# An LRU layer whose first three blocks share their chunks, with the adaLN sums dealt out between the matmuls

## The chip, the cores and the metric

The kernel runs on one core of a Trainium2 chip. The metric is the device time of one execution in microseconds (us), as the median of several runs. "Engines" are TensorE (PE), VectorE (DVE), ScalarE (ACT), GpSimd (POOL) and SyncE (SP, which here only issues transfers).

## What is computed

The model has two layers over 1024 latent tokens (D = 1024); the first also reads 256 context tokens. Layer 0 mixes tokens with a bidirectional gated linear recurrence (RG-LRU), layer 1 with long convolutions (Hyena); each is followed by a squared-ReLU MLP. Every sub-layer has an RMS norm with shift, scale and gate from the condition vector (adaLN). The change lies in layer 0 and in the start of the program:

```python
mod = cond @ ada_w[i] + ada_b[i]          # six vectors of 1024: j = 0..5
u = rms_norm(x, g) * (1 + scale) + shift
z = u @ w_in + b_in                        # 1024 x 2048
gate = gelu(z[..., :W])                    # "Z"
xl = row_conv(z[..., W:], conv_w, conv_b)  # "X", and the same for the context
r = sigmoid(xl @ w_a + b_a); i = sigmoid(xl @ w_i + b_i)   # "U", two directions, 4 heads of 256
log_a = -8 * r * softplus(-lam)
a = exp(log_a); bx = sqrt(-expm1(2 * log_a)) * i * xl      # "A"
h = linear_scan(a, bx, h0)                 # "S", forward and backward
y = ((h_f + h_b) * gate) @ w_out + b_out   # "Y"
h = sin(freq * (h @ fw + fb))              # Hyena's filter network, three steps, then h @ fw4
```

## The kernel before

**Precision.** Each fp32 product is made from a high and a low part of both operands, in three matmuls (`mm3`, lines L133 to L135). A weight block of 128x1024 is loaded by `load` (L111) into a buffer `raw`, ACT casts it to `whi` (L113), DVE subtracts to get `wlo` (L115). There are two `raw` buffers.

**Blocks.** Channels go in 8 blocks of 128, as four heads h with two halves m. The list `TOKENS` names the work by letter and block. `X` multiplies the normed input with one weight block, adds the convolution on DVE (L485) and splits the result into `xh` (ACT, L505) and `xl` (DVE, L507). `Z` makes the gelu gate. `U` makes the four sigmoid gates of one block from both halves of a head. `A` makes tanh and exp on ACT and the products on DVE and POOL. `S` takes the square roots, runs two scans on DVE (L588 into the tile `hf`, L591), combines them with the gate on POOL (L590, L592, L594), and writes `hf` to DRAM as `yd` (L596). There is one `hf` buffer.

**Sums.** `E` makes one of the six adaLN vectors (j = 2, 3, 4): eight loads `eraw` of 128x1024 (L615, in the two `raw` buffers), eight multiply-adds on DVE into `eacc` (L617, L619; `eacc` lies in the buffer of `hf`), and 8 matmuls of one column to sum over partitions (L622, each shown as two by the profile). In the list before, each of the three stands as one token between two blocks: `E20` ahead of Z00, `E30` ahead of U00, `E40` ahead of A00.

**Order.** A scheduler places the instructions of all tokens on the engines from its own estimates; within an engine, work is done in the placed order. All loads, and the writes `yd`, stand in SP's one queue. ACT's activations that need a table follow each other in program order (`table`).

**Start.** The program first makes the Hyena filter's features (sines, L302 to L312), the two adaLN vectors j = 0, 1 that the first norm needs (`ada_first`: 16 loads, 32 matmuls, L172), the norm's statistics of the three chunks (two of 512 latent columns, one of 256 context columns), and then scales and splits each chunk (L256 to L260). It also splits the filter network's last weight `fw4` and writes the parts to DRAM (`w4d`), from where the MLP part of layer 0 fetches them again.

Of the kernel before, what the change touches and what calls it, by code (L numbers as in the profile page):

```python
# [46 lines left out]
def tile_block(ctx: ExitStack, tc: tile.TileContext, a, out, dbg=None):  # L47
# [47 lines left out]
    w4d = dram.tile([4, P, 2, 512], F32, name="w4d")  # L95
# [190 lines left out]
    def filter_pos(fp, fb, aside):  # L286
# [13 lines left out]
        for n in range(3):  # L300
# [12 lines left out]
            aside(n)  # L313
        tap("fh3", h)
# [8 lines left out]
        hp = fp.tile([P, 16, 4, 32], F32, tag="hp", name="hp")  # L323
# [11 lines left out]
        for n, t in enumerate(split(fb, "hps", hp.rearrange("p g j t -> p (g j t)"), [P, 2048], 1, "v")):  # L335
            nc.sync.dma_start(hpd[:, :, n].rearrange("g p c -> p g c"), t.bitcast(F32).rearrange("p (g c) -> p g c", g=16))

    def filter_w4(fp, fb):
        fw4 = fp.tile([P, 2048], F32, tag="fw4", name="fw4")
        nc.sync.dma_start(fw4, a["fw4"])  # L340
        for n, t in enumerate(split(fb, "w4s", fw4, [P, 2048], 1)):
            nc.sync.dma_start(w4d[:, :, n].rearrange("u p c -> p u c"), t.bitcast(F32).rearrange("p (u c) -> p u c", u=4))

    def filters(fp):
# [78 lines left out]
    def x_load(pool):  # L423
        xt = []
        for c, src, o, n in ((0, "xT", 0, 512), (1, "xT", 512, 512), (2, "ctxT", 0, TC)):
            xt.append([pool.tile([P, n], F32, tag=f"x{c}{k}", name=nm("xl"), bufs=1) for k in range(NT)])
            for k in range(NT):
                nc.sync.dma_start(xt[c][k], a[src][k * P:(k + 1) * P, o:o + n])
        return xt

    TOKENS = ("X00 X01 E20 Z00 E30 U00 E40 A00 X10 S00 Z01 U01 A01 X11 S01 "
# [4 lines left out]
    def lru(load, open_x, npool, close_n, xt, rs):  # L436
# [6 lines left out]
        with ExitStack() as st:  # L443
# [30 lines left out]
            for tag, dt, w, n in (("z", F32, T + TC, 1), ("xc", F32, T + TC, 3), ("g", F32, T, 2), ("R", F32, T + TC, 2), ("I", F32, T + TC, 2),  # L474
                                  ("xl2", F32R, T + TC, 1), ("T", F32, T + TC, 2), ("hf", F32, T, 1)):
                lt.tile([P, w], dt, tag=tag, name=nm(tag), bufs=n)
# [14 lines left out]
            def X(h, m):  # L491
# [3 lines left out]
                for c in (0, 1, 2) if dt < 2 else (2, 0, 1):  # L495
# [3 lines left out]
                    nc.scalar.activation(z[:, cols[c]], p, AF.Identity, bias=vcol("lru_b_in", 8 + dt))  # L499
                x_ = lt.tile([P, T + TC], F32, tag="xc", name=nm("xc"), bufs=3)  # L500
# [9 lines left out]

            def Z(h, m):
# [18 lines left out]
            def U(h, m):  # L530
# [4 lines left out]
                for e in range(2):  # L535
                    pcx = None
                    tl = []
                    for ai in range(2):
# [14 lines left out]
                        tl.append(r)  # L553
                    rs_.append(tl)
# [55 lines left out]
            def E(j, _):  # L610

                acc = lt.tile([P, T], F32, tag="hf", name=nm("eacc"), bufs=1)
                for k in range(NT):
# [775 lines left out]
```

## Time and profile before

| | us |
|---|---|
| median of 3 runs | 2873.65 (2871.66 to 2874.5) |
| the profiled execution | 2870.54 |
| its span, first to last instruction | 2868.8 |
| PE busy | 2680.0 (93%) |
| DVE busy | 1605.5 (56%) |
| ACT busy | 1098.6 (38%) |

The span is what the profile's rows divide; the profiled execution's own time lies 1.74 us above it, and 3.11 us below the median. Busy shares are means over the whole program: the stages of layer 0 that the change touches fill the first tenth of it, and have to be read by themselves.

### The profile page before, as it was taken

How to read it: one execution, taken by the hardware profiler on the slowest of the kernel's cores; microseconds unless marked ns; L12 is line 12 of the kernel's file. 1: busy time of each engine (PE TensorE's matmuls, PEld its weight loads, DVE VectorE, ACT ScalarE, POOL GpSimd, SP SyncE). 2: the span in 40 equal slices, each digit the busy share in tenths (PEclk: the TensorE clock that was granted, in tenths of full speed). 3: DMA queues.
4: the chain of work that ended last, by engine and by line, in shares of the span. 5: the costliest groups of instructions: out<-in, count | busy, mean ns of one | idle time of the engine just before them, and what ended most of it. 6: DMA issues, size and time to landing. Idle time of an engine off the chain costs nothing.

```text
span 2868.8 us, 29759 instructions
## 1 busy us (share of the span) xinstructions
PE 2680.0 (93%) x11298; PEld 2071.4 (72%) x11298; DVE 1605.5 (56%) x2193; ACT 1098.6 (38%) x1670; POOL 245.2 (9%) x154
## 2 busy tenths in 40 slices
PE   6789889999999999999999997778799999999998
PEld 1677777788777777788787763334488888888887
DVE  7666575875555555444833368768576333333336
ACT  6457667542333233322522244444434211122213
POOL 0223432100000000000100021112001000000000
PEclk8799999999999999999999999998899999999999
DMA  8431123344444434322313254455321111111112
GB/s 304 125 111 44 52 66 121 102 145 133 121 114 138 122 114 138 100 68 63 123 52 118 67 159 122 134 159 169 120 87 45 52 52 44 52 44 52 51 46 96
DMA packets 121794, 288.60 MB, mean 101 GB/s; under 512 B 11883, under 2 KB 28269, under 8 KB 121395
## 3 DMA queue, kind: packets, MB, share of 16 engines
q1 hardware_dynamic: 116578, 275.42, 31.6%
q0 software_dynamic: 3344, 9.18, 1.0%
q10 hardware_dynamic: 1728, 2.10, 0.2%
q8 instruction: 89, 1.46, 0.2%
q14 instruction: 55, 0.44, 0.0%
HBM read 215.08 MB, written 37.75 MB: 88 GB/s over the span
## 4 chain that ended last, share of the span: by engine, by line
PE 72%; DVE 11%; DMA 9%; ACT 6%; issue 2%; SPq 0%; POOL 0%; DVEq 0%; ACTq 0%; POOLq 0%
PE ps L152 52%; PE ps L134 4%; PE ps L133 4%; PE ps L135 4%; DMA e<-big 3%; DMA adaw<-in_ada_w_dram 2%; PE ps L396 2%; PE ps L928 1%; DVE xc L485 1%; DMA big<-e 1%; DMA eraw<-in_ada_w_dram 1%; DVE hf L588 1%; PE ps L822 1%; PE ps L947 1%; ACT r L525 1%
## 5 line engine op out<-in xcount | busy, mean ns | idle before, releaser
L152 PE MATMUL ps<-u,whi 128*128 128x512 f32 x2696 | 734.7, 394 | 0.0
L113 ACT CAST whi<-raw 128x1024 fp32r<-128x1024 f32 x206 | 216.3, 1050 | 1113.5 <-PE ps L152 1007.4
L152 PEld LDWEIGHTS ps<-u,whi 128*128 128x128 f32 x2696 | 505.1, 188 | 113.5 <-issue 7.4
L115 DVE TENSOR_TENSOR wlo<-raw,whi 128x1024 fp32r<-128x1024 f32 x206 | 261.9, 1271 | 467.8 <-ACT whi L113 467.0
L152 PE MATMUL ps<-u,wlo 128*128 128x512 f32 x1348 | 418.9, 390 | 0.0
L152 PE MATMUL ps<-hh,whi 128*128 128x512 f32 x896 | 296.7, 409 | 0.0
L152 PEld LDWEIGHTS ps<-u,wlo 128*128 128x128 f32 x1348 | 253.1, 188 | 53.0 <-DVE wlo L115 0.7
L152 PE MATMUL ps<-hh,wlo 128*128 128x512 f32 x896 | 282.1, 390 | 0.0
L152 PE MATMUL ps<-hl,whi 128*128 128x512 f32 x896 | 280.5, 390 | 0.0
L152 PEld LDWEIGHTS ps<-hh,whi 128*128 128x128 f32 x896 | 168.4, 188 | 51.3 <-issue 17.3
L134 PE MATMUL ps<-u,whi 128*128 128x512 f32 (+1 forms) x508 | 195.2, 385 | 3.5 <-POOL u L260 2.9
L133 PE MATMUL ps<-u,whi 128*128 128x512 f32 (+1 forms) x508 | 186.9, 385 | 11.5 <-ACT u L259 11.5
L745 DVE SCALAR_TENSOR_TENSOR big<-ps,mod,big 128x512 f32<-128x512 f32 (+1 forms) x132 | 91.7, 731 | 185.3 <-PE ps L152 177.7
L135 PE MATMUL ps<-u,wlo 128*128 128x512 f32 (+1 forms) x508 | 193.0, 382 | 1.8 <-DVE wlo L115 1.8
L152 PEld LDWEIGHTS ps<-hl,whi 128*128 128x128 f32 x896 | 168.3, 188 | 36.1 <-issue 1.0
L152 PEld LDWEIGHTS ps<-hh,wlo 128*128 128x128 f32 x896 | 168.2, 188 | 34.9
L745 DVE SCALAR_TENSOR_TENSOR x<-ps,mod,x 128x512 f32<-128x512 f32 x128 | 91.3, 746 | 145.1 <-PE ps L152 137.2
L195 DVE SCALAR_TENSOR_TENSOR acc<-adaw,cond,acc 128x512 f32<-128x512 f32 x98 | 73.6, 751 | 93.1 <-DMA adaw<-in_ada_w_dram 92.2
L260 POOL TENSOR_TENSOR u<-nu,u 128x512 fp32r<-128x512 f32 x24 | 33.9, 1413 | 1021.8 <-ACT u L259 1012.6
L133 PEld LDWEIGHTS ps<-u,whi 128*128 128x128 f32 x508 | 97.8, 193 | 29.9 <-ACT u L259 12.2
L134 PEld LDWEIGHTS ps<-u,whi 128*128 128x128 f32 x508 | 97.9, 193 | 25.4 <-POOL u L260 6.0
L135 PEld LDWEIGHTS ps<-u,wlo 128*128 128x128 f32 x508 | 97.4, 192 | 20.1 <-DVE wlo L115 3.0
(242 smaller groups left out, 4051.2 us busy)
## 6 DMA issues: line engine op xcount, KB each, us to landing
raw<-in_mlp_w_dram SPq DMA_DIRECT2D x136, 512.0 KB
adaw<-in_ada_w_dram SPq DMA_DIRECT2D x112, 256.0 KB
fd<-fe SPq DMA_DIRECT2D x64, 256.0 KB
big<-e SPq DMA_DIRECT2D x64, 256.0 KB
ft<-fd SPq DMA_DIRECT2D x64, 256.0 KB
e<-big SPq DMA_DIRECT2D x64, 256.0 KB
eraw<-in_ada_w_dram SPq DMA_DIRECT2D x24, 512.0 KB
raw<-in_hy_w_in_dram SPq DMA_DIRECT2D x24, 512.0 KB
```

The source lines that it names most:

```text
L113: lsplit[0] = nc.scalar.copy(hi, raw)
L115: lsplit[1] = nc.vector.tensor_tensor(lo, raw, hi.bitcast(F32), op=ALU.subtract)
L133: first = pin(nc.tensor.matmul(ps, wh, rh, start=start, stop=False))
L134: pin(nc.tensor.matmul(ps, wh, rl, start=False, stop=False))
L135: pin(nc.tensor.matmul(ps, wl, rh, start=False, stop=stop))
L152: nc.tensor.matmul(pp[c], x, y[c][k], start=first, stop=last)
L195: nc.vector.scalar_tensor_tensor(acc, w, s, acc, op0=ALU.mult, op1=ALU.add)
L260: applied[k % 2] = (nc.vector if k % 2 else nc.gpsimd).tensor_tensor(ul[k], u, uh[k].bitcast(F32), op=ALU.subtract)
L396: nc.tensor.matmul(p2, mf[:, 1 if g == 0 else 0], st.pop(("ht", i)), start=True, stop=True)
L485: eng.scalar_tensor_tensor(ov[:, :, so], zv[:, :, si], vcol("lru_conv_w", 8 * tap_ + dt), ov[:, :, so], op0=ALU.mult, op1=ALU.add)
L525: ins = nc.scalar.activation(*args, **kw)
L745: nc.vector.scalar_tensor_tensor(xs[m][:, cs], ps[:, :n], g2[:, m:m + 1], xs[m][:, cs], op0=ALU.mult, op1=ALU.add)
```

## The change

- The first three blocks, X00, X01 and Z00, become one token `B`: the three weight blocks are loaded ahead, and for each chunk the matmuls of the three blocks alternate. The context's X follow last.
- Each `E` becomes eight single steps. `estep()` stands after each chunk of an X or Z, after each pair of gates in U, and once after B; it issues the next step of those that are due. The eight steps of j = 2 are due from the start, those of j = 3 after S00, those of j = 4 after S01; what is left before an S is issued there.
- X puts the context's chunk first for all blocks.
- At the start, x is loaded ahead of the adaLN weights, statistics and scaling are written chunk by chunk, and the matrix of filter features (`filter_mat`) is assembled behind the norm, its low part on POOL.
- `fw4` is no longer split at the start; `fetch` in the MLP loads the raw quarter and splits it there.

The core of the diff (lines of the changed kernel are shifted by up to 60):

```diff
@@ -332,14 +334,13 @@
                 for j in range(4):
                     eng = nc.scalar.copy if j % 2 else nc.vector.tensor_copy
                     eng(dst[:, :, m, j, 16 * half:16 * half + 16], src[:, :, m, j, :])
-        for n, t in enumerate(split(fb, "hps", hp.rearrange("p g j t -> p (g j t)"), [P, 2048], 1, "v")):
+        hph = fp.tile([P, 2048], F32R, tag="hph", name="hph")
+        for q in range(4):
+            cs = slice(512 * q, 512 * q + 512)
+            nc.scalar.copy(hph[:, cs], hpr[:, cs].bitcast(F32))
+            nc.gpsimd.tensor_tensor(hpr[:, cs], hpr[:, cs].bitcast(F32), hph[:, cs].bitcast(F32), op=ALU.subtract)
+        for n, t in enumerate((hph, hpr)):
             nc.sync.dma_start(hpd[:, :, n].rearrange("g p c -> p g c"), t.bitcast(F32).rearrange("p (g c) -> p g c", g=16))
-
-    def filter_w4(fp, fb):
-        fw4 = fp.tile([P, 2048], F32, tag="fw4", name="fw4")
...
@@ -353,7 +354,10 @@

         def fetch(u):
             w = fp.tile([P, 2, 512], F32R, tag="w4", name=nm("w4"), bufs=2)
-            nc.sync.dma_start(w.bitcast(F32), w4d[u])
+            raw = fp.tile([P, 512], F32, tag="fe", name=nm("w4r"), bufs=2)
+            nc.sync.dma_start(raw, a["fw4"][:, u * 512:(u + 1) * 512])
+            nc.scalar.copy(w[:, 0], raw)
+            nc.vector.tensor_tensor(w[:, 1], raw, w[:, 0].bitcast(F32), op=ALU.subtract)
             st["w4", u] = w

...
-    TOKENS = ("X00 X01 E20 Z00 E30 U00 E40 A00 X10 S00 Z01 U01 A01 X11 S01 "
...
+    TOKENS = ("B00 U00 A00 X10 S00 Z01 U01 A01 X11 S01 "
               "Z10 U10 A10 X20 S10 Z11 U11 A11 X21 S11 "
...
@@ -446,9 +450,24 @@
                 uh[c], ul[c] = ([utile(s_, c) for _ in range(NT)] for s_ in "hl")
             both = [utile("", 2) for _ in range(NT)]
             uh[2], ul[2] = [t[:, :TC] for t in both], [t[:, TC:] for t in both]
-            for c, n in ((0, 512), (1, 512), (2, TC)):
+            xt = x_tiles(npool)
+            with ExitStack() as fst:
+                fs = fst.enter_context(tc.tile_pool(name="fs", bufs=1, reuse_waits="tile"))
+                first = ada_first(fs, wp_[0])
+                h = filter_pos(fs)
+                x_load(xt, 0)
+                for step in first:
+                    step()
+                make_scale(scl[:, 0], vcols("norm_g", 0, 8), mod[:, 0, 1])
+                make_scale(sclc, vcols("norm_g", 0, 8), modc[:, 1])
+                w0 = [load(a["lru_w_in"][m]) for m in (8, 9, 0)]
+                for c in (1, 2):
+                    x_load(xt, c)
                 with tc.high_priority():
-                    norm_apply(npool, lambda k: xt[c][k], rs[c], n, scl[:, 0] if c < 2 else sclc, mod[:, 0, 0] if c < 2 else modc[:, 0], uh[c], ul[c], True)
+                    for c, n in ((0, 512), (1, 512), (2, TC)):
+                        r = norm_stats(npool, lambda k: xt[c][k], n, npool)
+                        norm_apply(npool, lambda k: xt[c][k], r, n, scl[:, 0] if c < 2 else sclc, mod[:, 0, 0] if c < 2 else modc[:, 0], uh[c], ul[c], True)
+                filter_mat(fs, h)
             close_n()

             sp8 = up.tile([P, 2, 16], F32, name="sp8")
...
                 dt = 2 * h + m
                 w = load(a["lru_w_in"][8 + dt])
                 z = lt.tile([P, T + TC], F32, tag="z", name=nm("z"), bufs=1)
-                for c in (0, 1, 2) if dt < 2 else (2, 0, 1):
+                for c in (2, 0, 1):
                     ps = psum()
                     p = ps if c < 2 else ps[:, :TC]
                     gemm(p, w, 0, uh[c], ul[c], range(NT), NT)
                     nc.scalar.activation(z[:, cols[c]], p, AF.Identity, bias=vcol("lru_b_in", 8 + dt))
+                    estep()
+                mix(h, m, z)
+
...
+            def B(h, m):
+
+                zz = [lt.tile([P, T + TC], F32, tag=t, name=nm("z"), bufs=n) for t, n in (("z", 1), ("xc", 3))]
+                g = lt.tile([P, T], F32, tag="g", name=nm("g"), bufs=2)
+                GT[0, 0] = g
+                for c in range(3):
+                    n = 3 if c < 2 else 2
+                    pp = [psum() for _ in range(n)]
+                    pp = [p if c < 2 else p[:, :TC] for p in pp]
+                    for k in range(NT):
+                        for i in range(n):
+                            gemm(pp[i], w0[i], 0, uh[c], ul[c], [k], NT)
+                    for i in range(2):
+                        nc.scalar.activation(zz[i][:, cols[c]], pp[i], AF.Identity, bias=vcol("lru_b_in", 8 + i))
+                    if c < 2:
+                        table(g[:, cols[c]], pp[2], AF.Gelu_apprx_tanh, bias=vcol("lru_b_in", 0))
+                for i in range(2):
+                    mix(0, i, zz[i])
+                estep()
+
...
@@ -516,6 +560,7 @@
                     ps = psum()
                     gemm(ps, w, 0, uh[c], ul[c], range(NT), NT)
                     table(g[:, cols[c]], ps, AF.Gelu_apprx_tanh, bias=vcol("lru_b_in", dt))
+                    estep()
                 GT[h, m] = g


...
                         tl.append(r)
+                        estep()
                     rs_.append(tl)
                 RW[h, m] = rs_
...
-            def E(j, _):
-
-                acc = lt.tile([P, T], F32, tag="hf", name=nm("eacc"), bufs=1)
-                for k in range(NT):
-                    w = wp_[0].tile([P, 1024], F32, tag="raw", name=nm("eraw"), bufs=2)
-                    nc.sync.dma_start(w, a["ada_w"][0, k * P:(k + 1) * P, j * D:(j + 1) * D])
-                    if k == 0:
-                        nc.vector.tensor_scalar(acc, w, cond[:, 0, k:k + 1], None, op0=ALU.mult)
-                    else:
-                        nc.vector.scalar_tensor_tensor(acc, w, cond[:, 0, k:k + 1], acc, op0=ALU.mult, op1=ALU.add)
+
+            eacc = {}
+
+            def E(j, k):
+                if k == 0:
+                    eacc[j] = lt.tile([P, T], F32, tag="hf", name=nm("eacc"), bufs=1)
+                acc = eacc[j]
+                w = wp_[0].tile([P, 1024], F32, tag="raw", name=nm("eraw"), bufs=2)
+                nc.sync.dma_start(w, a["ada_w"][0, k * P:(k + 1) * P, j * D:(j + 1) * D])
+                if k == 0:
+                    nc.vector.tensor_scalar(acc, w, cond[:, 0, k:k + 1], None, op0=ALU.mult)
+                else:
+                    nc.vector.scalar_tensor_tensor(acc, w, cond[:, 0, k:k + 1], acc, op0=ALU.mult, op1=ALU.add)
+                if k < NT - 1:
+                    return
                 ps = psum_st()
                 for t in range(8):
                     nc.tensor.matmul(ps[:, t:t + 1], acc[:, t * P:(t + 1) * P], ones[:, 0:1], start=True, stop=True)
@@ -624,8 +675,20 @@
                 if j == 4:
                     make_scale(scl[:, 1], vcols("norm_g", 8, 8), mod[:, 0, 4])

-            for tok in TOKENS.split():
-                dict(E=E, X=X, Z=Z, U=U, A=A, S=S, Y=Y)[tok[0]](int(tok[1]), int(tok[2]))
+            etodo = [(2, k) for k in range(NT)]
+
+            def estep():
+                if etodo:
+                    E(*etodo.pop(0))
+
+            for i, tok in enumerate(TOKENS.split()):
+
+                if tok[0] == "S":
+                    while etodo:
+                        estep()
+                dict(B=B, X=X, Z=Z, U=U, A=A, S=S, Y=Y)[tok[0]](int(tok[1]), int(tok[2]))
+                if tok in ("S00", "S01"):
+                    etodo.extend((3 + int(tok[2]), k) for k in range(NT))

         xs = open_x()
         late = [2, 3, 4, 5, 6, 7, 0, 1]
```

What the scheduler makes of it, at three places that matter below.

**Place 1: the loads and the write of S00.** SP's queue before, from the weights of X10 on (in order those of X10, Z01, U01's gates, X11, Z10 and U10's gates, `raw_1161` to `raw_1615`, then `yd_78`, the result of S00):

```order
L111 DMA raw_1161<-in_lru_w_in_dram 128x1024
L111 DMA raw_1270<-in_lru_w_in_dram 128x1024
L111 DMA raw_1329<-in_lru_w_g_dram 128x1024
L111 DMA raw_1447<-in_lru_w_in_dram 128x1024
L111 DMA raw_1556<-in_lru_w_in_dram 128x1024
L111 DMA raw_1615<-in_lru_w_g_dram 128x1024
L596 DMA yd_78<-hf_1263 128x1024
L111 DMA raw_1733<-in_lru_w_in_dram 128x1024
```

SP's queue of the changed kernel, from the weights of Z01 on (`yd_77` is the result of S00, `raw_1257` the gate weights of U01, `eraw` the loads of the sum j = 3, `raw_1387` the weights of X11):

```order
L110 DMA raw_1191<-in_lru_w_in_dram 128x1024
L664 DMA eraw_1225<-in_ada_w_dram 128x1024
L664 DMA eraw_1254<-in_ada_w_dram 128x1024
L642 DMA yd_77<-hf_1184 128x1024
L110 DMA raw_1257<-in_lru_w_g_dram 128x1024
L664 DMA eraw_1288<-in_ada_w_dram 128x1024
L664 DMA eraw_1315<-in_ada_w_dram 128x1024
L664 DMA eraw_1343<-in_ada_w_dram 128x1024
L664 DMA eraw_1370<-in_ada_w_dram 128x1024
L110 DMA raw_1387<-in_lru_w_in_dram 128x1024
L664 DMA eraw_1420<-in_ada_w_dram 128x1024
```

The gate weights of U01 (`raw_1329` before, `raw_1257` now) stood ahead of the write of S00's result, with three more weight blocks between; now they stand behind that write and behind two loads of the sum.

On DVE, the scans of S00 before (`xl_1257` belongs to X10, the two `wlo` to the weights of X11 and Z10):

```order
L586 SCALAR_TENSOR_TENSOR T_1147<-r_1013,r_1038 128x256
L115 TENSOR_TENSOR wlo_1451<-raw_1447,whi_1449 128x1024
L588 SCALAR_TENSOR_TENSOR hf_1263<-r_1013,T_1147,r_1038 128x1024
L485 SCALAR_TENSOR_TENSOR xc_1246<-z_1167,vec,xc_1246 128x16x62
L591 SCALAR_TENSOR_TENSOR T_1149<-r_1062,r_1087 128x1280
L485 SCALAR_TENSOR_TENSOR xc_1246<-z_1167,vec,xc_1246 128x16x63 x2
L507 TENSOR_TENSOR xl_1257<-xc_1246,xh_1255 128x1280
L115 TENSOR_TENSOR wlo_1560<-raw_1556,whi_1558 128x1024
```

and in the changed kernel, the same scans, up to the gate weights of U01 (`wlo_1261`):

```order
L631 TENSOR_TENSOR r_967<-r_967,T_1049 128x1280
L632 SCALAR_TENSOR_TENSOR T_1049<-r_939,r_967 128x256
L634 SCALAR_TENSOR_TENSOR hf_1184<-r_939,T_1049,r_967 128x1024
L504 SCALAR_TENSOR_TENSOR xc_1167<-z_1069,vec,xc_1167 128x16x62
L504 SCALAR_TENSOR_TENSOR xc_1167<-z_1069,vec,xc_1167 128x16x63
L637 SCALAR_TENSOR_TENSOR T_1051<-r_994,r_1022 128x1280
L504 SCALAR_TENSOR_TENSOR xc_1167<-z_1069,vec,xc_1167 128x16x63
L531 TENSOR_TENSOR xl_1178<-xc_1167,xh_1176 128x1280
L666 TENSOR_SCALAR eacc_1224<-eraw_1225,cond 128x1024
L668 SCALAR_TENSOR_TENSOR eacc_1224<-eraw_1254,cond,eacc_1224 128x1024
L114 TENSOR_TENSOR wlo_1261<-raw_1257,whi_1259 128x1024
```

The first step of the sum (`eacc_1224`) has come between the scans and the split of U01's gate weights; `eraw_1225` is in the buffer into which `raw_1257` goes, and `eacc_1224` in the one that `hf_1184` has.

**Place 2: the end of a U.** ACT's order before, at the end of U01 (`r` are the sigmoids, `T` the first tanh of A01, `whi_1617` the gate weights of U10):

```order
L525 ACTIVATE r_1409<-ps_1410,vec 128x512
L525 ACTIVATE r_1409<-ps_1418,vec 128x512
L113 CAST whi_1617<-raw_1615 128x1024
L525 ACTIVATE r_1409<-ps_1401,vec 128x256
L525 ACTIVATE T_1433<-r_1335,sp_633 128x1280
L525 ACTIVATE T_1435<-r_1384,sp_633 128x1280
```

and in the changed kernel at the same place (`whi_1514` are the weights of Z10):

```order
L570 ACTIVATE r_1346<-ps_1347,vec 128x512
L570 ACTIVATE r_1346<-ps_1355,vec 128x512
L112 CAST whi_1514<-raw_1512 128x1024
L570 ACTIVATE r_1346<-ps_1335,vec 128x256
L570 ACTIVATE T_1373<-r_1263,sp_643 128x1280
L570 ACTIVATE T_1375<-r_1318,sp_643 128x1280
```

In both, the cast of a weight block stands ahead of U01's last sigmoid and of A01's tanh. The load of that block was the fourth transfer on SP's queue behind Z01's weights (`raw_1270`); it is now the twelfth behind Z01's weights (`raw_1191`): the write of S00's result and all eight loads of the sum stand between.

**Place 3: the column sums of the first E.** PE's order before, at the end of X01 (`ps_839` are X01's context columns, `ps_920` and `ps_946` the first chunks of Z00):

```order
L133 MATMUL ps_839<-u_500,whi_782 128x256
L134 MATMUL ps_839<-u_500,whi_782 128x256
L135 MATMUL ps_839<-u_500,wlo_784 128x256
L622 MATMUL pst_903<-ones,eacc_878 128x1 x8
L133 MATMUL ps_920<-u_461,whi_915 128x512
L134 MATMUL ps_920<-u_469,whi_915 128x512
L133 MATMUL ps_946<-u_477,whi_915 128x512
```

and in the changed kernel, in U00 (`ps_995` and `ps_940` are gates of U00):

```order
L133 MATMUL ps_995<-xl_914,whi_935 128x512
L134 MATMUL ps_995<-xh_912,wlo_937 128x512
L132 MATMUL ps_995<-xh_925,whi_935 128x512
L673 MATMUL pst_1157<-ones,eacc_929 128x1 x3
L133 MATMUL ps_940<-xl_927,whi_935 128x512
L134 MATMUL ps_940<-xh_925,wlo_937 128x512
L133 MATMUL ps_948<-xl_927,whi_935 128x512
```

The sum j = 2 stood between two blocks; its matmuls now stand in two pieces among the gates of U00.

## Rows read from the trace of the kernel before

**Rows 1.** Which core: its span and mean granted clock.

```profile
core 0: 2868.8 us, clock 0.968
```

**Rows 2.** Busy time by stretch, each engine; PEclk; DMA share; GB/s.

```profile
77.20:107.60 30.40, 30.23 (x144) 24.97 (x144) 24.11 (x22) 16.75 (x34) 15.89 (x12) 0.92 0.26 77
107.60:159.20 51.60, 37.74 (x153) 31.29 (x152) 31.18 (x32) 18.06 (x24) 3.10 (x1) 0.77 0.61 186
159.20:212.40 53.20, 45.14 (x210) 38.24 (x211) 36.68 (x25) 32.30 (x38) 16.38 (x6) 0.90 0.29 92
212.40:258.50 46.10, 40.42 (x194) 33.81 (x193) 29.25 (x18) 30.14 (x35) 16.27 (x5) 0.93 0.14 46
```

**Rows 3.** Timeline of PE, 107 to 170 us: start, duration, work [idle before].

```profile
113.40 3.57 PE L622 MATMUL pst<-ones,eacc 128*128 128x1 f32 x16 [5.75 <-DVE eacc L619]
...
139.95 3.54 PE L622 MATMUL pst<-ones,eacc 128*128 128x1 f32 x16 [6.31 <-DVE eacc L619]
143.35 0.77 PE L133 MATMUL ps<-xh,whi 128*128 128x512 f32 x1
...
165.80 3.54 PE L622 MATMUL pst<-ones,eacc 128*128 128x1 f32 x16 [6.61 <-DVE eacc L619]
```

**Rows 4.** Timeline of ACT, 155 to 269 us.

```profile
158.52 0.69 ACT L525 ACTIVATE r<-ps,vec 128x512 f32<-128x512 f32 x1 [0.46 <-PE ps L135]
166.81 1.04 ACT L113 CAST whi<-raw 128x1024 fp32r<-128x1024 f32 x1 [7.60 <-DMA raw<-in_lru_w_in_dram]
...
168.13 2.61 ACT L525 ACTIVATE T<-r,sp 128x1280 f32<-128x1280 f32 x2
...
215.02 2.61 ACT L525 ACTIVATE T<-r,sp 128x1280 f32<-128x1280 f32 x2
...
261.78 2.61 ACT L525 ACTIVATE T<-r,sp 128x1280 f32<-128x1280 f32 x2
```

**Rows 5.** Timeline of ACT at the first main matmul.

```profile
64.48 10.68 ACT L258 ACTIVATE xl<-xl,mod,scl 128x512 f32<-128x512 f32 x15 [0.67 <-DVE scl L271]
...
76.05 1.12 ACT L259 CAST u<-xl 128x512 fp32r<-128x512 f32 x2
```

**Rows 6.** Timeline of PE, start of the program to first main matmul.

```profile
6.79 15.63 PE L172 MATMUL ps<-afw,cond 128*2 128x512 f32 x32 [0.44 <-DMA afw<-in_ada_w_dram]
...
77.22 0.80 PE L133 MATMUL ps<-u,whi 128*128 128x512 f32 x1 [11.54 <-ACT u L259]
```

**Rows 7.** Chain that ended last, 60 to 270 us: start, duration, what.

```profile
94.22 0.68 DVE eacc L617
...
137.06 4.34 DMA raw<-in_lru_w_g_dram
...
160.57 3.70 DMA eraw<-in_ada_w_dram
...
180.01 0.23 PE ps L134
```

**Rows 8.** SP's DMA issues, 105 to 260 us.

```profile
113.37 21.04 SPq L615 DMA_DIRECT2D eraw<-in_ada_w_dram  x8
...
190.22 0.33 SPq L111 DMA_DIRECT2D raw<-in_lru_w_g_dram  x1
203.10 0.33 SPq L596 DMA_DIRECT2D yd<-hf  x1
...
246.67 0.33 SPq L596 DMA_DIRECT2D yd<-hf  x1
```

**Rows 9.** DMA of tile yd, issue to landing.

```profile
DMA to landing us min/median/max: 2.9/5.1/7.2
```

**Rows 10.** DVE groups by form, 92 to 125 us.

```profile
L619 DVE SCALAR_TENSOR_TENSOR eacc<-eraw,cond,eacc 128x1024 f32<-128x1024 f32 x9 | 11.5, 1282 | 5.7 <-DMA eraw<-in_ada_w_dram 5.5 <-DVE xc L485 0.2
...
L617 DVE TENSOR_SCALAR eacc<-eraw,cond 128x1024 f32<-128x1024 f32 x2 | 1.5, 746 | 0.0
L507 DVE TENSOR_TENSOR xl<-xc,xh 128x1280 fp32r<-128x1280 f32 x1 | 1.5, 1485 | 0.0
```

More of the change, by code (lines that the diff above doesn't have):

```diff
@@ L420, in filters, with x_tiles, x_load @@
         return [lambda i=i: step(i) for i in range(len(steps) + LAG)]
[L423 to L426, printed above, removed]
-            for k in range(NT):
-                nc.sync.dma_start(xt[c][k], a[src][k * P:(k + 1) * P, o:o + n])
-        return xt
-    TOKENS = ("X00 X01 E20 Z00 E30 U00 E40 A00 X10 S00 Z01 U01 A01 X11 S01 "
+    def x_tiles(pool):
+        return [[pool.tile([P, n], F32, tag=f"x{c}{k}", name=nm("xl"), bufs=1) for k in range(NT)] for c, n in ((0, 512), (1, 512), (2, TC))]
+    def x_load(xt, c):
+        src, o, n = (("xT", 0, 512), ("xT", 512, 512), ("ctxT", 0, TC))[c]
+        for k in range(NT):
+            nc.sync.dma_start(xt[c][k], a[src][k * P:(k + 1) * P, o:o + n])
+    TOKENS = ("B00 U00 A00 X10 S00 Z01 U01 A01 X11 S01 "
               "Z10 U10 A10 X20 S10 Z11 U11 A11 X21 S11 "
@@ L434, in tile_block, with lru @@
               "Z30 U30 A30 Z31 U31 " + " ".join(f"Y{k}{c}" for k in range(6) for c in range(2)) + " S30 A31 S31")
-    def lru(load, open_x, npool, close_n, xt, rs):
+    def lru(load, open_x, npool, close_n):
         su = ExitStack()
@@ L473, in lru @@
             lt = st.enter_context(tc.tile_pool(name="lt", bufs=1, reuse_waits="tile"))
[L474 to L475 removed]
+            for tag, dt, w, n in (("hf", F32, T, 1), ("T", F32, T + TC, 2), ("xl2", F32R, T + TC, 1), ("I", F32, T + TC, 2), ("R", F32, T + TC, 2),
+                                  ("z", F32, T + TC, 1), ("xc", F32, T + TC, 3), ("g", F32, T, 2)):
                 lt.tile([P, w], dt, tag=tag, name=nm(tag), bufs=n)
@@ L509, in X @@
                 XC[h, m] = (x_, xh, xl)
+            def B(h, m):
[6 more added lines that the diff above has]
+                    pp = [p if c < 2 else p[:, :TC] for p in pp]
+                    for k in range(NT):
+                        for i in range(n):
[7 more added lines that the diff above has]
+                estep()
             def Z(h, m):
@@ L1148, in tile_block @@
     npool = npst.enter_context(tc.tile_pool(name="ln", bufs=1, side="right", reuse_waits="tile"))
-    rs = []
-    with ExitStack() as st:
-        fb = st.enter_context(tc.tile_pool(name="fb", bufs=1, reuse_waits="tile"))
-        fs = st.enter_context(tc.tile_pool(name="fs", bufs=1, reuse_waits="tile"))
-        first = ada_first(fs, wpool)
-        xt = []
-        def aside(n):
-            if n == 0:
-                for _ in range(8):
-                    first.pop(0)()
-                xt.extend(x_load(npool))
-            if n == 1:
-                for c, n_ in ((0, 512), (1, 512), (2, TC)):
-                    rs.append(norm_stats(npool, lambda k: xt[c][k], n_, npool))
-            if n == 2:
-                for _ in range(8):
-                    first.pop(0)()
-                filter_w4(fs, fb)
-        filter_pos(fs, fb, aside)
-        make_scale(scl[:, 0], vcols("norm_g", 0, 8), mod[:, 0, 1])
-        make_scale(sclc, vcols("norm_g", 0, 8), modc[:, 1])
-    xs, r0 = lru(load, open_x, npool, npst.close, xt, rs)
+    xs, r0 = lru(load, open_x, npool, npst.close)
     for k in range(NT):
```

16 lines of the change are left out of this document (7 added, 9 removed).

## The prediction

> **What bounds the kernel now.** I read the span first: 2868.8 us at a mean granted clock of 0.968 [rows 1]. That is almost full speed for the program as a whole, so a change in layer 0 can only show in layer 0. The table by stretch says the same: between 77.2 and 212.4 us, PE is granted 0.92, 0.77 and 0.90 of its speed and is busy 30.2 of 30.4, 37.7 of 51.6 and 45.1 of 53.2 us [rows 2]. Behind that, a round of one block takes 46 us and PE is busy 40 of them.
>
> Then I looked for what PE waits for. On its timeline the three sums stand out: each time PE idles 5.75, 6.31 and 6.61 us for the sum on DVE, and spends 3.5 us on its column sums [rows 3]. On ACT the third of them shows twice: U00's sigmoids end in a wait of 7.60 us for a weight block that stood behind the sum's loads, so that the tanh of A00 starts at 168.13 although U00's matmuls ended about 159.2 [rows 4]. After that the kernel has a beat: tanh at 168.13, 215.02 and 261.78, so 46.9 and 46.8 us a round [rows 4]. From a tanh to the write of the finished block SP shows 203.10 - 168.13 = 35.0 and 246.67 - 215.02 = 31.65 us [rows 4, 8]. That chain (tanh, exp, scans, POOL's products) is as long as two thirds of a round, and nothing waits for its end now: the gate weights of later blocks are issued before it (190.22 for those of U10, against 203.10 for the write) [rows 8].
>
> **The start: no gain.** Chunk by chunk, the first block could begin when one chunk is scaled. But ACT's new order still has 14 scalings ahead of the first cast, as before 15 of them, 10.68 us, stand ahead of the cast at 76.05 [rows 5]. PE now does the three filter matmuls ahead of the adaLN matmuls, of which one vector takes 15.63 us [rows 6]. With two vectors behind each other from about 28.5 us on (the filter's first two sines and eight squares lie ahead) they end at about 62, and scale is known at 65 to 68 with the DVE work in front, against 64.5 now, when the scalings begin [rows 5]. I take the first main matmul at 77.8 us, within 72 to 82, against 77.22 [rows 6]. Removing the load and the split of fw4 and its writes takes nothing off this path; the fetch in the MLP costs one cast and one subtraction per quarter on engines that idle there, taken as 0.5 us in all, with an upper end of 6 if the first pieces come late.
>
> **B and U00: 15 us gained.** B has 144 matmuls of 512 columns at 0.23 us [rows 7] and 48 of 256 columns at half of that: 38.5 us, and 2.5 more for a slow beginning as in the first stretch (30.4 us at 0.92 [rows 2]), so 41. U00 then needs xl of both X. On DVE these stand among the steps of the first sum, which share one buffer: one step starts 94.22 - 77.22 = 17 us after the first matmul now [rows 6, 7]; six more, each a load of 3.7 to 3.9 and a step of 1.28 [rows 7, 10], come to 17.7 + 6 x 5.2 = 49. One more step and two subtractions of 1.49 [rows 10] follow, so xl is complete at 52 to 57. I let U00 run from +54: its own 15.84 us (143.35 to 159.2 [rows 3, 4]) and the 3.54 of column sums that now lie inside [rows 3] end it at +73.5, so at 151.3 us; tanh of A00 at 152.9, since no load is late there. That is 168.13 - 152.9 = **15.2 us** sooner, with ends of 8 (first matmul late, xl at +57) and 21. It is what the three idle stretches and the column sums were worth, less what B loses waiting for xl.
>
> **U01 and U10: two new stalls.** The gate weights of U01 now stand on SP's queue behind the write of S00's result, and their buffer is free only when the first step of the second sum has run, whose accumulator is the one hf buffer: it waits until that write has landed (place 1). Counted from tanh of A00: write issued at +31 (the 31.65 of the later round less part of one wlo that is gone [rows 4, 8]), landed 2.9 later at least and 5.1 in the middle [rows 9], first step 0.75 [rows 10], so the gate load starts at g = +35. It lands after 3.7 to 4.3 [rows 7], the cast is 1.05, and U01's first matmul is at +40.5. PE has by then done X10 and Z01 and is idle some 15 us.
>
> Behind the late load, ACT's order holds more. The cast of Z10's weights stands ahead of U01's last sigmoid and so ahead of the next tanh (place 2). Those weights are the ninth load from g on in the two buffers; eight loads took 21.04 us when DVE was free for them [rows 8], so they land at g + 21 + 3.9, and with cast and sigmoid tanh of A01 starts at g + 27 = +62. U01 itself would be over earlier (5.5 to its first matmul, 16.2 of matmuls, 1.6 of sigmoid: g + 23.3). So the round is 62 us instead of 46.9: **15.2 us** lost. The third sum does the same to U10: its gate weights stand behind the write of S01, with the same accumulator: again 46.8 becomes 62. Together **+30.4**, each with ends of 11.5 and 18. What else waits behind the held instruction on DVE (the split of U01's weights, X11's convolution) needs U01 or X11's matmuls and is late by the same amount, not more. After the third sum the rounds are as before; its column sums add 3.5 us of PE in a round where PE idles 5 [rows 2].
>
> On the queue that holds the sigmoid, the trace shows ACT idle for 7.60 us with finished matmuls behind the cast [rows 4]. [...]
>
> On the loads' price, the rows show 3.7 to 4.3 us for 512 KB [rows 7]. [...]
>
> **Sum.** -15.2 + 30.4 + 0.5 for the fetch = +15.7 (the later first matmul is already in the 151.3). Against the profiled execution's 2870.54 that is 2886.2; it lay 3.11 under the median of its runs, so the median comes to **2889**. Its own range goes from 2879 to 2899.
>
> **Rivals.**
> - *Mild stalls.* Casts come in time, rounds end with U's matmuls: 2 x 11.5 - 15.2 = +8, 2882. For it speaks that the sums' loads might go faster than 2.63 us each; against it that ACT's order puts a cast ahead of the sigmoid.
> - *Heavier stalls.* The write lands 5 to 7 us after its issue [rows 9] and the sums' steps wait for each other on DVE behind scans: 18 a round and 12 gained early: +24, 2898.
> - *Balance.* The first matmul comes 5 us sooner, since scale is known when the second vector's loads allow it, and the rounds are mild: about +3, 2876, which can't be told from no change.
> - *Faster.* The result of S00 leaves early enough. The round is the write's issue plus 31 (4 to the load, 27 to tanh), so it falls under the 54.4 us at which two rounds eat the 15.2 only if the write is issued 23 us after tanh; at 16 there is no stall, and the whole early gain stays: 2858. The rows give 31.65 and 35.0 [rows 4, 8] and speak against it; what could shorten the chain is that POOL and DVE meet less and that fewer splits stand between the scans.
>
> **How the numbers follow.** Likeliest 0.50, mild 0.17, heavier 0.12, balance 0.11, faster 0.10. A difference of under 0.2%, 5.7 us, can't be told from none here. Slower by more takes the likeliest, the heavier and nearly all of the mild one; the mild one's lower end and the balance are "same"; so 0.75, 0.14, 0.11. The range goes from 2872, inside the balance, to 2902, above the heavier: it leaves out the faster case and a tenth of the rest.
>
> **What the changed profile would show.** Right: no idle PE before a column sum of the first E; first main matmul near 77.8 and tanh of A00 near 153; on SP the write of S00 and the gate load of U01 3 to 5 us after it; PE idle about 15 us before U01's and U10's first matmul with the cast of their weights as releaser; tanh near 153, 215 and 277. Wrong: a gate load well ahead of the write, a round under 55 us, a first main matmul under 70, or a tanh of A00 after 160.

## The result, and the profile after

The changed kernel takes 2891.62 us (median of 4 runs, 2885.65 to 2893.03) against 2873.03 for the kernel before (median of 4 runs, 2871.66 to 2874.5): a ratio of 1.0062, 95% interval 1.0047 to 1.0077, so 18.6 us slower; 2889 was predicted. Its profiled execution has a span of 2891.3 us, 22.5 more than before. The two profiled executions thus lie 3.9 us further apart than the medians.

PE's timeline of the changed kernel, at its four longest idle times (start, duration, work, idle before and its releaser):

```profile
73.65 0.80 PE L132 MATMUL ps<-u,whi 128*128 128x512 f32 x1 [11.25 <-ACT u L258]
...
127.22 0.79 PE L132 MATMUL ps<-xh,whi 128*128 128x512 f32 x1 [12.04 <-ACT xh L529]
...
189.24 0.80 PE L132 MATMUL ps<-xh,whi 128*128 128x512 f32 x1 [17.95 <-ACT whi L112]
...
252.43 0.80 PE L132 MATMUL ps<-xh,whi 128*128 128x512 f32 x1 [19.77 <-ACT whi L112]
```

No idle time stands before a column sum any more, where three of 5.75 to 6.61 us did [rows 3]. In their place are one of 12.04 before U00, which waits for both convolutions, and two of 17.95 and 19.77 before U01 and U10, whose releaser is the cast of their gate weights.

ACT's timeline at the ends of U00, U01, U10 and U11 (T is the tanh that begins a round's chain; a round goes from one tanh to the next):

```profile
148.84 2.61 ACT L570 ACTIVATE T<-r,sp 128x1280 f32<-128x1280 f32 x2
...
188.15 1.04 ACT L112 CAST whi<-raw 128x1024 fp32r<-128x1024 f32 x1 [10.94 <-DMA raw<-in_lru_w_g_dram]
...
212.06 1.05 ACT L112 CAST whi<-raw 128x1024 fp32r<-128x1024 f32 x1 [5.78 <-DMA raw<-in_lru_w_in_dram]
213.02 0.47 ACT L570 ACTIVATE r<-ps,vec 128x256 f32<-128x256 f32 x1
213.38 2.61 ACT L570 ACTIVATE T<-r,sp 128x1280 f32<-128x1280 f32 x2
...
276.54 2.60 ACT L570 ACTIVATE T<-r,sp 128x1280 f32<-128x1280 f32 x2
...
322.75 2.61 ACT L570 ACTIVATE T<-r,sp 128x1280 f32<-128x1280 f32 x2
```

Against [rows 4], the first tanh is 19.3 us earlier (148.84 for 168.13), the two rounds after it take 64.5 and 63.2 us instead of 46.9 and 46.8, and the next is back at 46.2. So 19.29 us are gained and 17.65 + 16.40 = 34.05 lost, which leaves +14.8 at the third tanh. The row at 212.06 shows the second half of each loss: ACT waits 5.78 us for Z10's weights, with U01's last sigmoid and the tanh behind that cast.

The chain that ended last, of the changed kernel, shows the first half link by link:

```profile
174.25 3.24 POOL hf L638
...
177.56 3.48 POOL hf L640
...
181.05 2.60 DMA yd<-hf
...
183.73 0.77 DVE eacc L666
...
184.51 3.61 DMA raw<-in_lru_w_g_dram
...
188.15 1.05 ACT whi L112
```

POOL ends hf, the write lands 2.60 us later, at once the sum's first step runs, at once the gate weights are loaded, and PE's row of 189.24 follows the cast.

The table by stretch, in the stretches of [rows 2] (length; busy us of PE, PEld, DVE, ACT and POOL with their instructions; granted clock; DMA share; GB/s):

```profile
77.20:107.60 30.40, 30.40 (x132) 25.03 (x132) 19.23 (x24) 15.82 (x33) 12.86 (x10) 0.97 0.12 35
107.60:159.20 51.60, 39.08 (x213) 33.63 (x212) 26.93 (x29) 29.58 (x38) 5.94 (x2) 0.87 0.31 93
159.20:212.40 53.20, 35.25 (x166) 29.45 (x165) 32.16 (x21) 19.07 (x24) 13.53 (x4) 0.81 0.33 104
212.40:258.50 46.10, 26.33 (x117) 21.66 (x116) 31.05 (x22) 23.35 (x24) 13.12 (x4) 0.78 0.22 74
```

The granted clock was 0.87 for 0.77 in the stretch with the gaps before the sums, where PE is now idle for 12.5 us instead of 13.9, and 0.81 and 0.78 for 0.90 and 0.93 in the two with the new gaps, where it is idle for 17.95 and 19.77 us instead of 8.1 and 5.7.

Not all of the 22.5 us lies there. At the end of layer 0's mixing (about 540 us) the changed kernel is 16.6 us behind, at the start of layer 1's convolutions 15.5. Then the convolution stage, which computes the same, takes 5.4 us more, and the end of the program about 1.5 more. Rows of before and of after for it:

```profile
1667.20:2139.70 472.50, 387.12 (x1203) 223.88 (x1202) 347.54 (x500) 208.65 (x361) 72.17 (x61) 0.93 0.49 141
```

```profile
1682.80:2160.70 477.90, 386.84 (x1202) 224.00 (x1201) 349.08 (x500) 208.80 (x361) 71.64 (x59) 0.93 0.48 138
```

The engines' busy times agree within 1.6 us; the stage only waits more.

### The profile page after: what moved, and what is told of

Read it like the earlier page. It is cut to its first block, busy times and chain, and to the rows that moved or that the text cites. A ratio compares the mean times of both kernels' runs of the same rounds, so it can differ in the third digit from the quotient of the medians.

```text
span 2891.3 us, 29757 instructions
## 1 busy us (share of the span) xinstructions
PE 2670.1 (92%) x11298; PEld 2065.5 (71%) x11298; DVE 1604.4 (55%) x2194; ACT 1099.7 (38%) x1675; POOL 251.4 (9%) x158
## 3 DMA queue, kind: packets, MB, share of 16 engines
q8 instruction: 89, 1.46, 0.2%
## 4 chain that ended last, share of the span: by engine, by line
PE 75%; DVE 9%; DMA 8%; ACT 5%; issue 2%; POOL 1%; SPq 0%; DVEq 0%; ACTq 0%
PE ps L151 53%; PE ps L133 5%; PE ps L132 5%; PE ps L134 5%; DMA e<-big 3%; PE ps L400 2%; DMA eraw<-in_ada_w_dram 1%; PE ps L885 1%; PE ps L1010 1%; DMA big<-e 1%; PE ps L991 1%; DVE xc L504 1%; DMA adaw<-in_ada_w_dram 1%; DVE hf L634 1%; DVE t L1022 1%
## 5 line engine op out<-in xcount | busy, mean ns | idle before, releaser
L151 PEld LDWEIGHTS ps<-u,wlo 128*128 128x128 f32 x1348 | 253.1, 188 | 53.1 <-DVE wlo L114 0.8
L151 PEld LDWEIGHTS ps<-hl,whi 128*128 128x128 f32 x896 | 168.3, 188 | 36.1 <-issue 1.0
L151 PEld LDWEIGHTS ps<-hh,wlo 128*128 128x128 f32 x896 | 168.3, 188 | 34.9
L132 PE MATMUL ps<-xh,whi 128*128 128x512 f32 (+1 forms) x192 | 76.0, 414 | 76.9 <-ACT whi L112 37.7
```

Source lines behind the costliest of these rows:

```text
L132: first = pin(nc.tensor.matmul(ps, wh, rh, start=start, stop=False))
L151: nc.tensor.matmul(pp[c], x, y[c][k], start=first, stop=last)
```

## The experiments

Theory A is the prediction's: the sum's first step waits for the write of S, the gate load waits behind it, and a late cast holds the tanh. Against it stood B (the sums' 16 extra loads and steps in those rounds do it, whatever they wait for) and C (the gate load's place behind the write on SP's queue does it). Each ratio is to the kernel before as measured beside that run (its medians there lie between 2871.24 and 2873.52); "less than the changed kernel" compares with the 2891.62 above.

**1. The accumulator out of hf's buffer.**

```diff
-                    eacc[j] = lt.tile([P, T], F32, tag="hf", name=nm("eacc"), bufs=1)
+                    eacc[j] = wp_[0].tile([P, 1024], F32R, tag="lo", name=nm("eacc")).bitcast(F32)
```

> The sums' accumulator moves out of the buffer of hf (into one of the three wlo buffers); all else as changed. Theory A (the first step of a sum waits for the write of S's result, and U's gate load behind it): nothing holds the gate loads any more, PE's idle times of 18 and 19.8 us before U01 and U10 fall under 3, the rounds from tanh to tanh go from 64.5 and 63.2 to 46 to 50, so 28 to 35 us less than the changed kernel: 2856 to 2864, faster than before. Rival B (the sums' loads themselves, 16 more in the two raw buffers in these two rounds, are what makes the gate weights late): the rounds stay above 58, 2880 to 2892.

Measured: 2870.15 us, ratio to before 0.9993 (0.9984 to 1.0002), so 21 us less than the changed kernel, short of what A expected. Tanh stands at 150.15, 200.90, 255.26 and 298.88: rounds of 50.8 and 54.4. Of the 34 us lost, 22.6 were the accumulator's wait (127.7 for two rounds falls to 105.1); 11.5 over before's two rounds remain. By PE's rows they are B's; whether it has a part in them that the accumulator now takes one of the three wlo buffers, the run doesn't tell:

```profile
195.45 0.98 PE L673 MATMUL pst<-ones,eacc 128*128 128x1 f32 x4 [6.95 <-DVE eacc L668]
```

```profile
238.91 0.80 PE L132 MATMUL ps<-xh,whi 128*128 128x512 f32 x1 [9.86 <-ACT xh L529]
```

PE waits for the sum itself ahead of its column matmuls, and for X11's convolution, among whose taps the sum's steps stand on DVE.

**2. The gate weights loaded ahead of the sum, the accumulator left where it was.**

```diff
                 w = load(a["lru_w_in"][dt])
+                if (h, m) in EARLY:
+                    GW[h, m] = load(a["lru_w_g"][h, m])
...
-                w = load(a["lru_w_g"][h, m])
+                w = GW.pop((h, m), None) or load(a["lru_w_g"][h, m])
```

> The gate weights of U01 and U10 are loaded with Z's weights, ahead of the sum's steps; the sums still wait for the write of S. Theory A: U01 and U10 start on time, what stays late are the weights of X11 and Z10, which stand behind the sum: PE idles some 7 us before X11 or Z10, rounds of 46 to 52, 22 to 33 us less than the changed kernel: 2858 to 2870. Rival B (the sums' loads as such): the same loads still have to pass through the two buffers in the round, so it stays above 58 a round and above 2880.

Measured: 2877.22, ratio 1.0015 (1.0006 to 1.0024), 14 us less than the changed kernel, and a miss. U01 starts on time and the first round takes 40.4 us, but the second 73.0. X11's and Z10's weights now stand behind the waiting sum, and that costs more than forecast. PE waits for X11's, and ACT's tanh again for a Z's:

```profile
200.75 0.58 PE L132 MATMUL ps<-u,whi 128*128 128x256 f32 x1 [11.68 <-ACT whi L112]
```

```profile
261.19 1.05 ACT L112 CAST whi<-raw 128x1024 fp32r<-128x1024 f32 x1 [5.74 <-DMA raw<-in_lru_w_in_dram]
262.14 0.47 ACT L573 ACTIVATE r<-ps,vec 128x256 f32<-128x256 f32 x1
```

The wait for the write moves from one load to the next behind it; it is not a matter of the gate weights alone.

**3. The cast of a Z's weights behind the last sigmoid of the U before.**

```diff
             lsplit[0] = nc.scalar.copy(hi, raw)
+            if behind:
+                tc.add_manual_dep(lsplit[0].ins, behind, NOSYNC, reason="order")
...
-                w = load(a["lru_w_in"][dt])
+                w = load(a["lru_w_in"][dt], behind=usig[0])
```

> On ACT, the cast of a Z's weights is ordered behind the last sigmoid of the U before; loads and sums as changed. Theory A says that of each long round some 6.5 us is tanh waiting behind this cast (206.7 against 213.4 and 269.7 against 276.5): the rounds come to 58 and 57, the kernel to 2878 (2874 to 2882). If the cast only delays what would be late anyway (Z's weights), the rounds stay 62 to 65 and the time within 3 us of the changed kernel's 2891.

Measured: 2873.37, ratio 1.0005 (0.9996 to 1.0015), 18 us less than the changed kernel. The two rounds take 58.7 and 58.9, as forecast:

```profile
207.37 0.47 ACT L572 ACTIVATE r<-ps,vec 128x256 f32<-128x256 f32 x1 [1.95 <-PE ps L136]
207.74 2.61 ACT L572 ACTIVATE T<-r,sp 128x1280 f32<-128x1280 f32 x2
210.88 1.05 ACT L112 CAST whi<-raw 128x1024 fp32r<-128x1024 f32 x1 [0.53 <-DMA raw<-in_lru_w_in_dram]
```

The tanh comes ahead of the weights that it stood behind, 5.6 us earlier than in the changed kernel. Two things were not forecast. The third round takes 50.7 us, 4.5 more than in the changed kernel, because ACT waits for the late weights behind the tanh now, ahead of the round's exp, which comes 11.5 us behind the tanh instead of 5.2:

```profile
271.15 1.05 ACT L112 CAST whi<-raw 128x1024 fp32r<-128x1024 f32 x1 [1.86 <-DMA raw<-in_lru_w_in_dram]
...
275.84 1.05 ACT L112 CAST whi<-raw 128x1024 fp32r<-128x1024 f32 x1 [3.27 <-DMA raw<-in_lru_w_g_dram]
```

Over the three rounds 5.6 us are gained (168.3 for 173.9). And the rounds after them, in which nothing is late, fall to 42.7 and 39.4 us. Run 8 takes that up.

**4. The writes of S's results issued by POOL.**

```diff
-                (nc.sync if dt < 6 else nc.gpsimd).dma_start(yd[dt], hf)
+                nc.gpsimd.dma_start(yd[dt], hf)
```

> All writes of S's results are issued by POOL, so that they do not stand on SP's queue; the accumulator still shares hf's buffer. Theory A (the wait is the accumulator's, until the write has landed): no gain, the gate loads are still issued after the first step of the sum, rounds 63 to 68, 2890 to 2898. Rival C (the place behind the write on SP's queue is what makes the gate load late): gate loads 20 us and more earlier, rounds under 55, 2862 to 2875.

Measured: 2889.97, ratio 1.0071 (1.0055 to 1.0088), no gain; rounds of 64.7 and 63.9. The chain is the same with no write on SP's queue:

```profile
180.76 3.08 DMA yd<-hf
...
183.93 0.77 DVE eacc L666
184.69 0.02 issue
184.71 3.55 DMA raw<-in_lru_w_g_dram
```

C falls: the gate load waits for the accumulator, not for its place behind the write.

**5. Without B** (`"X00 X01 Z00 U00 A00 ..."` in place of `"B00 U00 A00 ..."`; X as before otherwise, so all blocks begin with the context).

> The three first blocks one after the other again (X00 X01 Z00), all else as changed, the sums dealt out. The changed kernel has its tanh of A00 at 148.8, with PE idle 12 us between B and U00 because both convolutions end late. If the early gain comes from dealing the sums (theory A), it stays without B: X00's convolution lies beside X01 and Z00, U00 follows at once, tanh of A00 at 142 to 150, the two long rounds as before: 2884 to 2893. If B is what gains it (rival), tanh of A00 comes at 160 or later: 2902 or more.

Measured: 2887.21, ratio 1.0052 (1.0037 to 1.0067). Tanh of A00 stands at 147.64 although the first main matmul, which has to wait for the context's norm, comes only at 87.85; PE hardly idles from there to U01 (0.27 us). B itself gains nothing: without it this tanh is 1.2 us earlier. What gains is dealing out the sums, two of which now come behind A00; with the sums whole and in their old order, run 9 has this tanh at 158.41.

**6. The dropped DRAM tensor kept.**

```diff
+    w4d = dram.tile([4, P, 2, 512], F32, name="w4d")
     fd = dram.tile([4, 16, P, 512], F32, name="fd")
...
+    nc.sync.dma_start(w4d[0][:, 0, 0:128], ident)
```

> The changed kernel with the dropped DRAM tensor w4d still there (64 KB of it written once at the start, never read), so that all other DRAM tensors lie at their addresses of before. In the changed kernel and in all four variants so far the convolution stage of layer 1, whose work is the same, takes 3 to 5 us more than before. If the addresses make that, the time falls by 3 to 5 us: 2887; if not, it stays within 2 us of 2891.

Measured: 2897.43, ratio 1.0089 (1.0074 to 1.0104), a miss in the other direction. Tanh of A00 came 4.5 us later, with the 64 KB write on SP's queue at 3.04 us, among the first loads of x. The convolution stage was not shorter: it lost 6.8 us against before. So giving the tensors their old places doesn't take its waits away (no run shows the addresses themselves).

**7. The edits of runs 1, 2 and 3 together.**

> Three edits together on the changed kernel: accumulator out of hf's buffer, gate weights of U01 and U10 loaded with Z's, the casts of Z's weights behind U's last sigmoid. By theory A no wait for the write, the sums' place or the cast is left in these rounds; what may remain is PE waiting some 5 us for a sum ahead of its column matmuls: rounds 46 to 52, then as in the run with the cast behind (42.7 and 39.4): 2850 to 2864. If the sums' loads as such make the rounds long, 2868 or more.

Measured: 2855.94, ratio 0.9945 (0.9929 to 0.9962). The time is as forecast, the second round longer: rounds of 46.7 and 55.2, then 46.6, 43.5 and 39.4. The excess of the second is again the sum's steps among X11's taps: PE waits 10.25 us for its xh.

**8. The cast behind the sigmoid, on the kernel before.** The same edit as in run 3.

> The kernel before, with the casts of Z's weights ordered behind the last sigmoid of the U before; nothing else. On the changed kernel this edit also made the later rounds shorter, where no load is late. If that is the edit itself (a cast of 1 us ahead of the sigmoid, and the work behind tanh), the kernel before gains 4 to 10 us: 2863 to 2869. If it was only the recovery from late loads, it stays within 2 us of 2872.

Measured: 2854.92, ratio 0.9942 (0.9927 to 0.9956), 16 us less than before, more than expected. The reasons stand in rows of before that the prediction does not use. The first are those ahead of tanh of A01 [rows 4]:

```profile
211.67 0.69 ACT L525 ACTIVATE r<-ps,vec 128x512 f32<-128x512 f32 x1 [0.65 <-PE ps L135]
213.70 1.05 ACT L113 CAST whi<-raw 128x1024 fp32r<-128x1024 f32 x1 [1.34 <-PE ps L134]
214.66 0.47 ACT L525 ACTIVATE r<-ps,vec 128x256 f32<-128x256 f32 x1
```

The releaser of that cast, of U10's gate weights (place 2), is a matmul: the cast waits 1.34 us until PE gives a whi buffer free, and the last sigmoid, behind it, starts 2.99 us after the one before. With the order changed, two casts stand behind the tanh, and a round ends so:

```profile
292.53 0.69 ACT L527 ACTIVATE r<-ps,vec 128x512 f32<-128x512 f32 x1 [0.65 <-PE ps L137]
294.68 0.47 ACT L527 ACTIVATE r<-ps,vec 128x256 f32<-128x256 f32 x1 [1.46 <-PE ps L137]
295.05 2.61 ACT L527 ACTIVATE T<-r,sp 128x1280 f32<-128x1280 f32 x2
297.56 1.98 ACT L113 CAST whi<-raw 128x1024 fp32r<-128x1024 f32 x2
```

The sigmoid starts 2.15 us after the one before: it still waits 1.46 for PE, so this part is worth 0.84 us a round, which is all that the first round gains. The larger part lies on DVE. In the second round before, the split of Z11's weights, whose cast waited 3.09 us for PE, stands ahead of X20's xl:

```profile
244.35 3.38 DVE L115 TENSOR_TENSOR wlo<-raw,whi 128x1024 fp32r<-128x1024 f32 x1
247.65 1.48 DVE L507 TENSOR_TENSOR xl<-xc,xh 128x1280 fp32r<-128x1280 f32 x1
```

In run 8 cast and split come behind the next tanh, and xl starts 29.65 us after its round's tanh (212.07) instead of 32.63:

```profile
241.72 1.46 DVE L509 TENSOR_TENSOR xl<-xc,xh 128x1280 fp32r<-128x1280 f32 x1
```

Rounds fall from 46.9, 46.8, 44.9, 47.0 and 45.0 to 46.1, 43.6, 39.4, 43.5 and 39.4. At 39.4 PE has hardly any idle time left, by an estimate: X, Z and U are 144 matmuls of 512 columns and 48 of 256, which start 0.23 us [rows 7] and 0.12 us apart (110.22 to 113.58 us of the changed kernel's trace) where PE doesn't wait, 38.9 us.

**9. The new start alone**, blocks and whole sums in before's order (`"X00 X01 E20 Z00 E30 U00 E40 A00 ..."`).

> The changed kernel's start (x first, norm by chunks, filter matrix behind it, the raw fetch of fw4), but blocks and whole sums in the order of before. If the start brings nothing by itself (theory A), the first main matmul comes at 73 to 78, the three idle stretches of 6 us before the column sums are back, tanh of A00 at 164 to 169, rounds of 46.8: 2868 to 2875. If the start is what gained early (rival), tanh of A00 at 155 or less and 2860 or less.

Measured: 2870.29, ratio 0.9990 (0.9980 to 1.0000). First main matmul at 73.05, tanh of A00 at 158.41, outside both forecasts. But the third sum's column matmuls now follow behind it, after 10.19 us of idle PE:

```profile
168.19 0.99 PE L672 MATMUL pst<-ones,eacc 128*128 128x1 f32 x4 [10.19 <-DVE eacc L667]
```

So the first round takes 56.9, and tanh of A01 is at 215.27, as before (215.02).

**10 and 11. All sums ahead of S00**, without B, with the latent chunks first in X00 and X01 and run 3's cast. Run 10 deals out j = 2 at one step a chunk and the rest at two, run 11 two from the start.

```diff
-            etodo = [(2, k) for k in range(NT)]
+            etodo = [(j, k) for j in (2, 3, 4) for k in range(NT)]
...
-                if etodo:
-                    E(*etodo.pop(0))
+                for _ in range(1 if len(etodo) > 16 else 2):
+                    if etodo:
+                        E(*etodo.pop(0))
```

> All three sums dealt out ahead of S00, so that none lies in a round: blocks one after the other with latent chunks first, sum j = 2 at one step a chunk and the other two at two, accumulators in turn in hf's buffer and a wlo buffer, casts of Z's weights behind U's last sigmoid. By theory A no step meets a write of S, rounds of 46, 43.6 and 39.4 as in the kernel before with the cast behind, and tanh of A00 at 140 to 152 instead of 166: 2832 to 2846. If the steps crowded together make the weights late by themselves, tanh of A00 at 160 or more and 2850 or more.

> As the run before, with two steps a chunk from the start, so that the second block's weights stand behind six loads of the sum: PE idles 5 to 12 us before X01, tanh of A00 at 145 to 160: 2835 to 2856.

Measured: 2849.53, ratio 0.9923 (0.9908 to 0.9938), and 2854.92, ratio 0.9940 (0.9924 to 0.9957). Run 10 lies between its two forecasts, run 11 within its range. Run 10's tanh of A00 is at 153.03; its first round has 58.6 us, because PE waits for the third sum:

```profile
178.81 3.55 PE L675 MATMUL pst<-ones,eacc 128*128 128x1 f32 x16 [10.71 <-DVE eacc L670]
```

After it, rounds are 42.7 and 39.4. In run 11 X01's weights are late by 14.6 us, more than expected.

**12. The third sum's column matmuls behind Z01**, its accumulator in a wlo buffer, else as run 10, but for the other two accumulators, which have changed places as well (the first sum's now in a wlo buffer, the second's in hf's; the expectation doesn't name this).

> As the run with all sums ahead of S00 (one step a chunk, then two), but the third sum's accumulator lies in a wlo buffer and its column matmuls stand behind Z01 instead of ahead of it, where PE idled 10.7 us. If only their place in PE's order made the idle time, it goes: 2838 to 2843. If Z01's weights, which stand behind the same loads on SP's queue, are as late as the sum, PE waits for them instead and gains the 3.5 us of the column matmuls at most: 2845 to 2851.

Measured: 2835.05, ratio 0.9864 (0.9848 to 0.9881), better than both cases. Z01's weights were late by 5.06 us only, not by the sum's 10.7:

```profile
161.65 0.80 PE L134 MATMUL ps<-u,whi 128*128 128x512 f32 x1 [5.06 <-ACT whi L112]
```

Tanh of A00 came 8.6 us earlier as well, most of it because PE no longer waits for X01's weights (5.95 us in run 10). That lies ahead of the matmuls that were moved, and whether the exchanged accumulators made it was not tested. This version is 38 us faster than the kernel before.

## Why the prediction was right

- **The start.** "No gain" was nearly so: the first main matmul came at 73.65, not 77.8, 3.6 us before its old time and within the stated 72 to 82. Run 9 shows that the start alone is worth nothing that can be told, since a later wait takes its gain back.
- **B and U00.** B took 41.5 us (41), U00's first matmul came 53.6 us after B's (54), tanh of A00 at +75.2 (75.1). The early gain was 19.3 instead of 15.2; the difference is the first matmul's. Run 5 settles one point that the prediction left open: it is dealing out the sums that gains, not B.
- **The stalls.** Write issued 32.2 us after tanh (31), landed in 2.60 (2.9 at least), gate load at +35.7 (35), U01's first matmul at +40.4 (40.5), PE idle 17.95 (15). Runs 1 and 4 show that this wait is the accumulator's; run 3 that the cast ahead of the sigmoid adds to each round (64.5 and 63.2 with it, 58.7 and 58.9 without), though 4.5 of these 10.1 us come back in the third.
- **The rounds' price** was the mis-sized term of the stalls. The sum has the ninth load 21 us behind g, after "eight loads took 21.04 us". But that row [rows 8] goes from the first issue to the eighth, which is seven intervals of some 2.96 us and not eight of 2.63; the ninth comes after eight of them, at about g + 23.7. It was issued at g + 23.9 (the row below, less 184.51). So tanh came at g + 28.9 instead of g + 27, and 17.7 and 16.4 were lost where 15.2 each stood. That the early first matmul made up for this is luck: +14.8 against +15.2 at the third tanh.

```profile
208.42 0.33 SPq L110 DMA_DIRECT2D raw<-in_lru_w_in_dram  x1
```

- **Not in the sum** is what follows the third tanh. In the profile the rest of layer 0's mixing adds 1.8 us to the +14.8, layer 0's MLP with the fetch takes 1.1 off (0.5 more stood in the sum), layer 1's convolution stage adds 5.4 and the end of the program about 1.5. By the medians only 18.6 of the profile's 22.5 us are there, 3 above the sum's 15.7; in which of these stages the profiled executions differ from the median ones isn't known. In the twelve runs the convolution stage is 1 to 9 us longer than in the profile before, the only trace of that kernel. Run 8 is one of them, though its instructions there are those of before, PE's in the same order (a few neighbours on the other queues have changed places). Its medians bear out a part of that: it is 22.8 us ahead where the stage begins, and 16.3 us faster in all. What the stage waits for was not settled.
- **The steady beat.** The prediction took the old rounds of 46.8 as they are and didn't ask what sets them. Run 8 shows that 0.8 to 5.6 us of each came from where the casts and their splits stood; the two casts shown there waited 1.34 and 3.09 us for PE.
- **The rivals.** The mild one needs rounds that end with U's matmuls; run 3 made them, and at 58.7 and 58.9 they cost what that rival said (46.9 + 11.5), so the cast's place is what told the two apart (the 50.7 of the third round is not in that rival). The heavier one had the write land after 5 to 7 us; it took 2.60, and the rounds came near its 18 for another reason, the ninth load. The balance needed a first matmul 5 us sooner, of which 4.15 came, and mild rounds, which did not come. The faster one needed the write at +23; it came at +32.2. That POOL and DVE meet shows in the trace of before: the split of a wlo takes 1.22 us at 229.42, with POOL idle, and 3.38 at 244.35, beside POOL's product of 243.44 to 246.64. In the changed kernel they meet as well: S00's scan into hf takes 4.87 us there, beside POOL's product of 163.59 to 166.78, and 2.34 before, with POOL idle.

## What to carry to other kernels

Work that is dealt into small steps takes its buffers with it: before placing the steps, follow each step's accumulator and input buffer to whoever holds them last, a write to DRAM included (here the first step ran when it had landed, 2.60 us after its issue), and each queue to what stands behind the step. In ACT's order a cast for the next block belongs behind what the present block's chain needs, even when its data come in time: in the kernel before, two such casts waited 1.34 and 3.09 us for PE to give their output buffer free, a sigmoid and the tanh stood behind the first, and the split that followed the second stood ahead of X20's xl on DVE for 3.38 us. With the casts behind the sigmoid that kernel took 16 us less (run 8). When a time is added up from a row of several loads, count its intervals: eight issues are seven of them. When an idle time is taken away in one place, look at the next tanh (or whatever paces the loop), not at the idle time: run 9's first tanh came 9.7 us earlier, and one round later nothing was left of it.

## What the runs showed of the hardware that was not expected

A stage with the same instructions took 472.5 us in the profile before and 480.1 in run 8, with the busy times of the engines within 2.5 us; it began 23 us earlier there, and a few neighbouring transfers and vector operations had changed places. Whether it was one of the two, or the spread between executions, stays open. And in run 6, with a write of 64 KB at 3.04 us among the first loads of x, the first main matmul came 2.0 us later than in the changed kernel (75.67 for 73.65) and tanh of A00 4.5 us (153.33 for 148.84); how, and whether it was the write or the kept tensor, the run doesn't tell.
